# The decay of layer 2 without TensorE: turns by VectorE and memory, a broadcast load, a mask by GpSimd

## The chip, the cores and the metric

The kernel runs on one core of a Trainium2 chip. The metric is the device time of one execution in microseconds (us), taken as the median of several runs. TensorE multiplies matrices into PSUM banks; VectorE, ScalarE and GpSimd work on rows of up to 128 partitions; SyncE (SP) and GpSimd issue loads and stores. In the profile these are PE, DVE, ACT, POOL and SP. Each engine takes its instructions in a fixed order.

## The reference

The reference is a decoder trunk of two layers on 256 tokens of width 1024. Layer 1 is a sparse attention; layer 2, which the change touches, is a chunkwise mLSTM with 8 heads, q and k of 128 and v of 256 per head. What matters here is how its gates weigh the scores:

```python
i_pre = (gi + gate_b[0]).astype(f32).transpose(0, 2, 1)
log_f = jax.nn.log_sigmoid((gf + gate_b[1]).astype(f32)).transpose(0, 2, 1)
b = jnp.cumsum(log_f.reshape(B, H, N, L), axis=-1)
log_d = jnp.where(causal, b[..., :, None] - b[..., None, :] + i_pre[..., None, :], -jnp.inf)
m_j = jnp.maximum(jnp.max(log_d, axis=-1), m_inter)
s = jnp.einsum('bhnjk,bhnsk->bhnjs', q, k) * jnp.exp(log_d - m_j[..., None])
h = num / jnp.maximum(jnp.abs(den), jnp.exp(-m_j))[..., None]
```

The kernel does not chunk: with F the running sum of log_f over all 256 tokens and g = i_pre − F, a key s weighs on a query j by exp(g[s] − M[j]) where M is the running maximum of g (from 0), and by 0 where s is later than j. The floor of the denominator is exp(−(M + F)).

## The kernel before

Tokens lie in two halves of 128. Every weight is loaded by SP's queue into ten buffers (`raw`), split by ScalarE (L164, `wh`, the rounded part) and VectorE (L169, `wl`, the rest), and multiplied by TensorE in three products. `WBUF = 6` pairs of split buffers are kept; a split waits until TensorE has finished with the pair it writes to. The order of each engine's instructions is set at build time by a planner that simulates a timeline and takes what has priority first; `tc.high_priority()` puts its block ahead, `keep_in_program_order` and `issue_after` fix an order.

Between the layers, `turn` (L1092) normalises the tokens and makes the first products of layer 2, among them the 16 gate columns, which VectorE copies to GT (L1240): 128 tokens on the partitions, per half 8 input gates and 8 forget gates. `layer2` (L1282) then does the decay, in rows of 8 partitions (one per head) and 256 tokens, all in one tile `rows` of the tag QK:
- TensorE turns GT into rows (L1332, four transposes); VectorE adds the biases (L1333, L1334).
- log_sigmoid by ScalarE (Abs, Exp, Ln: L1335 to L1338) and VectorE (L1337 to L1343), on 8 x 256.
- VectorE scans F and M and makes −M in two parts in nM (L1344 to L1349).
- TensorE turns g back to columns (L1351), copied to GF (L1352).
- For each head, in bank 2 or 3: TensorE broadcasts the row of −M to 128 partitions with a selecting matrix (L1357), adds the causal mask by two bf16 products with an identity (L1358, L1359); ScalarE writes exp of the sum, with g as its bias, to DT (L1360, L1361).
- M + F, its floor and exp(−(M + F)) (L1363 to L1365), turned to columns by TensorE (L1368).

Around it run the big products: v_unit (values of two heads or one), conv_unit (one convolution over 256 columns of q or k) and later heads. A conv_unit takes a bank from a cycle of six (6, 7, 4, 5, 0, 1), as v_unit does; ScalarE starts `conv` (two buffers, L1380), VectorE adds three shifted terms (L1385) and the end is

```python
            with self.tc.issue_after(last.ins):
                nc.scalar.activation(QK[:, 2 * c : 2 * c + 2], acc, AF.Silu)
```

so a Silu stands behind `last` on ScalarE, and QK, which has the tag of `rows`, is written only when `rows` is free. The order of units is v_unit(2, 2), conv_units 0, 4, 1, 5, v_unit(4, 2), conv_units 2, 6, v_unit(6, 1), conv_units 3, 7; then heads 0 and 1 (`head`, L1389), which read DT at L1395. `factor` (L1414) reads the second half of GF.

Of the kernel before, what the change touches and what calls it, by code (L numbers as in the profile page):

```python
# [7 lines left out]
F32 = mybir.dt.float32  # L8
# [15 lines left out]
class Kernel:  # L24
# [225 lines left out]
    def setup(self):  # L250
# [31 lines left out]
        self.bif = self.T(pc, [8, 2])  # L282
# [17 lines left out]
        self.mask = self.T(pc, [P, P], BF16)  # L300
        self.identb = self.T(pc, [P, P], BF16)
        self.selh = self.T(pc, [P, 8], F32R)
        nc.vector.tensor_copy(self.selh, self.ident[:, 32:40])
        self.identr = self.T(self.p1, [P, P], F32R)
        nc.vector.tensor_copy(self.identr, self.ident)
        nc.vector.tensor_copy(self.selh[0:8], self.ident[0:8, 0:8])

    def late_constants(self):
        g = self.nc.gpsimd
        g.memset(self.int1, 1)  # L310
        g.memset(self.intm, 0x7FFFFFFF)
        m32 = self.T(self.p1, [P, P])
        g.memset(m32, 0.0)
        g.affine_select(m32, m32, pattern=[[1, P]], compare_op=OP.is_ge, fill=-1e30, base=0, channel_multiplier=-1)
        g.tensor_copy(self.mask, m32)
        g.tensor_copy(self.identb, self.ident)
# [775 lines left out]
    def turn(self):  # L1092
# [146 lines left out]
        for a in range(2):  # L1239
            nc.vector.tensor_copy(GT[:, a], bs[a][:, 256:272])  # L1240
# [41 lines left out]
    def layer2(self):  # L1282
# [18 lines left out]
        mask, identb, selh = self.mask, self.identb, self.selh  # L1301
# [19 lines left out]
        rows = self.T(p2, [8, 9, SEQ], tag="QK")  # L1321
        gi, xf, e, u, sp, d, ones, Fc, M = [rows[:, n] for n in range(9)]
        nM = self.T(p2, [P, 384], F32R)
        GF = self.T(p2, [P, 2, 2, 8])
        g.memset(ones, 1.0)
        g.memset(nM.bitcast(F32), 0.0)
        bg, bt = self.bank(2), self.bank(3)
        with self.tc.high_priority():
            for a in range(2):
                for n in range(2):  # L1330
                    c = n * SEQ + a * P
                    nc.tensor.transpose(bg[0:8, c : c + P], GT[:, a, 8 * n : 8 * n + 8], ident)  # L1332
            nc.vector.tensor_scalar(xf, bg[0:8, SEQ:], self.bif[:, 1:2], None, op0=OP.add)  # L1333
            nc.vector.tensor_scalar(gi, bg[0:8, 0:SEQ], self.bif[:, 0:1], None, op0=OP.add)  # L1334
            nc.scalar.activation(e, xf, AF.Abs)  # L1335
            nc.scalar.activation(e, e, AF.Exp, scale=-1.0)
            nc.vector.tensor_scalar(u, e, 1.0, None, op0=OP.add)  # L1337
            nc.scalar.activation(sp, u, AF.Ln)  # L1338
            nc.vector.scalar_tensor_tensor(d, u, -1.0, e, op0=OP.add, op1=OP.subtract)
            nc.vector.reciprocal(u, u)  # L1340
            nc.vector.tensor_tensor(d, d, u, op=OP.mult)
            nc.vector.tensor_sub(sp, sp, d)
            nc.vector.scalar_tensor_tensor(sp, xf, 0.0, sp, op0=OP.min, op1=OP.subtract)  # L1343
            nc.vector.tensor_tensor_scan(Fc, ones, sp, 0.0, OP.mult, OP.add)  # L1344
            nc.vector.tensor_sub(gi, gi, Fc)
            nc.vector.tensor_tensor_scan(M, ones, gi, 0.0, OP.mult, OP.max)
            nc.vector.tensor_scalar(nM[0:8, 0:SEQ], M, -1.0, None, op0=OP.mult)
            nc.vector.scalar_tensor_tensor(nM[32:40, 0:SEQ], M, -1.0, nM[0:8, 0:SEQ].bitcast(F32), op0=OP.mult, op1=OP.subtract)
            nc.vector.tensor_copy(nM[0:40, SEQ:384], nM[0:40, P:SEQ].bitcast(F32))  # L1349
            for a in range(2):  # L1350
                nc.tensor.transpose(bt[:, 8 * a : 8 * a + 8], gi[:, a * P : a * P + P], ident[:8, :8])  # L1351
            nc.vector.tensor_copy(GF[:, 0].rearrange("p a h -> p (a h)"), bt[:, 0:16])  # L1352
        DT = self.T(p2, [P, 8, 384], tag="DT")
        with self.tc.high_priority():
            for h in range(8):
                b = self.bank(2 + h % 2)
                nc.tensor.matmul(b[:, 0:384], selh[:, h : h + 1].to_broadcast([P, P]), nM, start=True, stop=False, skip_group_check=True)  # L1357
                nc.tensor.matmul(b[:, 0:P], identb, mask, start=False, stop=False, skip_group_check=True)  # L1358
                nc.tensor.matmul(b[:, SEQ:384], identb, mask, start=False, stop=True, skip_group_check=True)  # L1359
                nc.scalar.activation(DT[:, h, 0:SEQ], b[:, 0:SEQ], AF.Exp, bias=GF[:, 0, 0, h : h + 1])  # L1360
                last = nc.scalar.activation(DT[:, h, SEQ:384], b[:, SEQ:384], AF.Exp, bias=GF[:, 0, 1, h : h + 1])  # L1361
        v_unit(2, 2)
        nc.vector.tensor_tensor(M, M, Fc, op=OP.add)  # L1363
        nc.vector.tensor_scalar(M, M, -88.0, None, op0=OP.max)
        last = nc.scalar.activation(M, M, AF.Exp, scale=-1.0)  # L1365
        b = self.bank(2)
        for a in range(2):
            nc.tensor.transpose(b[:, 8 * a : 8 * a + 8], M[:, a * P : a * P + P], ident[:8, :8])  # L1368
        nc.vector.tensor_copy(GF[:, 1].rearrange("p a h -> p (a h)"), b[:, 0:16])

# [43 lines left out]
        def factor(b4):  # L1414
            hs = slice(4 * b4, 4 * b4 + 4)
            S = lambda tag: self.T(p2, [P, 2, 4], tag=tag, bufs=2)
            dn, v = S("dn"), S("fv")
            nc.vector.scalar_tensor_tensor(dn, den[:, :, hs], -1.0, den[:, :, hs], op0=OP.mult, op1=OP.max)
            nc.vector.tensor_tensor(dn, dn, GF[:, 1, :, hs], op=OP.max)
            nc.vector.reciprocal(dn, dn)  # L1420
            nc.vector.tensor_tensor(v, ss[:, :, hs], dn, op=OP.mult)
            nc.vector.tensor_tensor(v, v, dn, op=OP.mult)
            nc.vector.tensor_scalar(v, v, 1.0 / 256, 1e-6, op0=OP.mult, op1=OP.add)
            y = self.rsqrt(pc, v.rearrange("p a h -> p (a h)"), 8)
            nc.vector.tensor_tensor(rf[:, :, hs], dn, y.rearrange("p (a h) -> p a h", a=2), op=OP.mult)
# [227 lines left out]
def layout(inputs):  # L1653
# [16 lines left out]
    out["gate_b"] = a["b_gate_b"][0].T  # L1670
# [25 lines left out]
```

## Time and profile before

| what | value |
|---|---|
| median of 3 runs | 427.54 us (427.27 to 427.9) |
| profiled execution, span from first to last instruction | 425.8 us (its only time on the page) |
| TensorE busy | 415.7 us, 98% |
| VectorE busy | 353.7 us, 83% |
| ScalarE busy | 272.0 us, 64% |
| GpSimd busy | 82.1 us, 19% |
| moved by DMA | 94.54 MB, 222 GB/s in the mean |

The span is what the profiler saw; the runs' time also holds what lies around it. Busy time of TensorE is modelled from pipelined matmuls, so that a busy share near 100% says that it was never without work, not that it ran at its peak.

### The profile page before, as it was taken

The numbers are of one execution on the slowest core, as the hardware profiler recorded it, in microseconds if no ns is written. First come the engines' busy times: TensorE is split into PE (matmuls) and PEld (weight loads), VectorE is DVE, ScalarE is ACT, GpSimd is POOL, SyncE is SP. The second block draws the span as 40 slices with busy tenths as digits, with TensorE's granted clock in tenths as the row PEclk, the third lists the DMA queues.
The fourth block names the chain that finished last, engine by engine and source line by source line (L and its number), as shares of the span: only waits on it lengthen the run. The fifth ranks groups of instructions, "written<-read, shape, count | busy, mean of one in ns | idle before, by whom it ended". The sixth has DMA issues, their size and how long they took to land.

```text
span 425.8 us, 7641 instructions
## 1 busy us (share of the span) xinstructions
PE 415.7 (98%) x2701; PEld 359.7 (84%) x2701; DVE 353.7 (83%) x747; ACT 272.0 (64%) x542; POOL 82.1 (19%) x127
## 2 busy tenths in 40 slices
PE   7999999999999999999999999999999999999994
PEld 4899998789778878888998899888888888888884
DVE  6999798999999998979983796889878997458553
ACT  5766693788978964668576865465456454555523
POOL 4000212364586740120000000000000350220000
PEclk9999999999999999999999999999999999999999
DMA  8999986973799678148754366558555687540002
GB/s 313 413 408 407 396 306 192 357 280 107 256 353 391 226 255 307 58 145 295 247 172 168 105 237 190 166 174 264 163 188 197 213 290 229 168 142 0 2 0 99
DMA packets 26886, 94.54 MB, mean 222 GB/s; under 512 B 3072, under 2 KB 3088, under 8 KB 26848
## 3 DMA queue, kind: packets, MB, share of 16 engines
q1 hardware_dynamic: 26208, 92.30, 61.6%
q0 software_dynamic: 352, 0.97, 0.7%
q10 hardware_dynamic: 288, 0.79, 0.5%
q8 instruction: 21, 0.34, 0.3%
q14 instruction: 17, 0.14, 0.1%
HBM read 93.00 MB, written 1.05 MB: 221 GB/s over the span
## 4 chain that ended last, share of the span: by engine, by line
PE 86%; issue 6%; DMA 2%; POOL 2%; DVE 2%; ACT 1%; SPq 1%; DVEq 0%; POOLq 0%; ACTq 0%
PE bank L550 10%; PE bank L548 10%; PE bank L549 10%; PE bank L442 8%; PE bank L1613 6%; PE bank L1611 6%; PE bank L1612 6%; PE bank L1524 5%; PE bank L1045 5%; PE bank L1167 3%; DMA Q<-in_columns 2%; PE bank L808 2%; PE bank L1404 2%; PE bank L825 2%; PE bank L763 2%
## 5 line engine op out<-in xcount | busy, mean ns | idle before, releaser
L169 DVE TENSOR_TENSOR wl<-raw,wh 128x1024 fp32r<-128x1024 f32 (+4 forms) x127 | 139.3, 1112 | 37.3 <-ACT wh L164 36.4
L164 ACT ACTIVATE wh<-raw 128x1024 fp32r<-128x1024 f32 (+4 forms) x127 | 119.4, 957 | 72.9 <-PE bank L550 31.8
L548 PE MATMUL bank<-wh,one 128*128 128x512 f32 (+1 forms) x208 | 76.8, 370 | 0.0
L549 PE MATMUL bank<-wl,one 128*128 128x512 f32 (+1 forms) x208 | 76.3, 367 | 0.0
L550 PE MATMUL bank<-wh,one 128*128 128x512 f32 (+1 forms) x208 | 76.3, 368 | 0.0
L1611 PE MATMUL bank<-one,wh 128*128 128x256 f32 x208 | 59.6, 287 | 0.0
L1613 PE MATMUL bank<-one,wl 128*128 128x256 f32 x208 | 59.2, 285 | 0.1
L1612 PE MATMUL bank<-one,wh 128*128 128x256 f32 x208 | 59.0, 284 | 0.0
L803 POOL TENSOR_SCALAR Pr<-Pr,f 128x128 f32<-128x128 f32 (+1 forms) x42 | 46.7, 1130 | 31.4 <-DVE f L797 25.1
L548 PEld LDWEIGHTS bank<-wh,one 128*128 128x128 f32 x208 | 39.2, 189 | 6.1 <-DVE tz L520 0.2
L550 PEld LDWEIGHTS bank<-wh,one 128*128 128x128 f32 x208 | 39.2, 188 | 6.1
L549 PEld LDWEIGHTS bank<-wl,one 128*128 128x128 f32 x208 | 39.2, 189 | 5.9
L1611 PEld LDWEIGHTS bank<-one,wh 128*128 128x128 f32 x208 | 39.7, 191 | 1.3 <-issue 0.8
L1613 PEld LDWEIGHTS bank<-one,wl 128*128 128x128 f32 x208 | 39.7, 191 | 0.5 <-DVE wl L169 0.3
L1612 PEld LDWEIGHTS bank<-one,wh 128*128 128x128 f32 x208 | 39.7, 191 | 0.1
L789 ACT ACTIVATE Pr<-Pr,mn 128x128 f32<-128x128 f32 (+1 forms) x64 | 28.2, 444 | 4.4 <-DVE mn L782 4.4
L442 PE MATMUL bank<-one,wh 128*128 128x256 f32 x224 | 29.8, 284 | 0.7 <-ACT one L416 0.4
L442 PEld LDWEIGHTS bank<-one,wh 128*128 128x128 f32 x224 | 28.1, 192 | 1.1 <-ACT one L416 0.6
L1487 POOL DMA_DIRECT2D DT<-in_final_g x1 | 0.6, 560 | 131.7 <-DVE pl L1399 131.7
L160 POOL TENSOR_TENSOR raw<-raw,gate 128x256 f32<-128x256 f32 x16 | 15.5, 976 | 47.8 <-DMA raw<-in_out_b 22.5
L1385 DVE SCALAR_TENSOR_TENSOR conv<-bank,one,conv 128x255 f32<-128x255 f32 (+2 forms) x48 | 20.2, 471 | 2.1 <-ACT conv L1380 2.1
L861 DVE CUSTOM_DVE_ANT_0 raw<-raw,one,one 128x1024 f32<-128x1024 f32 x16 | 21.1, 1331 | 0.0
(343 smaller groups left out, 813.6 us busy)
## 6 DMA issues: line engine op xcount, KB each, us to landing
raw<-in_wide SPq DMA_DIRECT2D x44, 512.0 KB, 4.1
raw<-in_units SPq DMA_DIRECT2D x18, 512.0 KB, 3.5
raw<-in_turn SPq DMA_DIRECT2D x16, 512.0 KB, 7.7
raw<-in_gates SPq DMA_DIRECT2D x16, 512.0 KB, 4.7
raw<-in_out_b SPq DMA_DIRECT2D x16, 512.0 KB, 3.8
raw<-in_start SPq DMA_DIRECT2D x8, 512.0 KB, 9.6
Q<-in_columns SPq DMA_DIRECT2D x8, 512.0 KB, 9.6
raw<-in_hidden SPq DMA_DIRECT2D x8, 512.0 KB, 4.2
```

The source lines that it names most:

```text
L164: self.nc.scalar.activation(v(hi), src, AF.Copy)
L169: self.nc.vector.tensor_sub(v(lo), src, v(hi).bitcast(F32))
L442: nc.tensor.matmul(out, w[:, ch * P : ch * P + P], h[:, kk], start=(kk == 0 and m == 0 and ch % 2 == 0), stop=(kk == 7 and m == 2), skip_g ...
L548: nc.tensor.matmul(out, self.hh[:, kk, sl], wh, start=first, stop=False, skip_group_check=True)
L549: nc.tensor.matmul(out, self.hh[:, kk, sl], wl, start=False, stop=False, skip_group_check=True)
L550: nc.tensor.matmul(out, self.hl[:, kk, sl], wh, start=False, stop=last, skip_group_check=True)
L789: nc.scalar.activation(v, v, AF.Exp, bias=mn[:, a, br, j : j + 1], scale=-1.0, accum_out=sm[:, a, br, j : j + 1])
L803: es[br].tensor_scalar(v, v, F[n][:, a, br, j : j + 1], None, op0=OP.mult)
L1045: ins = nc.tensor.matmul(out, l[:, sl], w[:, c0:c1], start=(k == 0 and m == 0), stop=(k == N - 1 and m == 2), skip_group_check=True)
L1611: nc.tensor.matmul(out, wh, self.hh[:, kk], start=first, stop=False, skip_group_check=skip)
L1612: nc.tensor.matmul(out, wh, self.hl[:, kk], start=False, stop=False, skip_group_check=skip)
L1613: nc.tensor.matmul(out, wl, self.hh[:, kk], start=False, stop=last, skip_group_check=skip)
```

## The change

The gates are biased when they leave PSUM (`bif`, the biases, is now loaded to all 128 partitions), and log_sigmoid is made while the tokens are still on the partitions, on 128 x 2 x 8, by GpSimd with Exp and Ln by ScalarE and one reciprocal by VectorE. VectorE's transpose turns blocks of 32 x 32; the blocks go to a scratch tensor in memory (`drawer`) and come back as rows by four loads. The scans stay on VectorE. g goes to memory (`store[0]`) and comes back in blocks for VectorE to turn into GF; −M goes to memory (`shelf`) and is loaded to all 128 partitions of DT. GpSimd writes −1e30 into the masked triangle of two column ranges of DT, and ScalarE takes the exponentials in place. exp(−(M + F)) goes to memory (`store[1]`) and comes back by blocks as g did. `last` is now the last exponential of DT. All new loads and stores are issued by GpSimd. The mask, its bf16 identity and the selecting matrix are no longer made.

```diff
-        self.bif = self.T(pc, [8, 2])
+        self.bif = self.T(pc, [P, 16])
...
-            nc.vector.tensor_copy(GT[:, a], bs[a][:, 256:272])
+            nc.vector.tensor_tensor(GT[:, a], bs[a][:, 256:272], self.bif, op=OP.add)
...
+        rows = self.T(p2, [8, 5, SEQ], tag="QK")
+        gi, xf, ones, Fc, M = [rows[:, n] for n in range(5)]
+        small = self.T(p2, [P, 5, 2, 8])
+        lf, e, u, sp, d = GT[:, :, 8:16], small[:, 0], small[:, 1], small[:, 2], small[:, 3]
+        nM = self.T(p2, [8, 384])
...
+            g.tensor_scalar(d, lf, 0.0, 2.0, op0=OP.min, op1=OP.mult)
+            g.tensor_tensor(d, d, lf, op=OP.subtract)
+            nc.scalar.activation(e, d, AF.Exp)
+            g.tensor_scalar(u, e, 1.0, None, op0=OP.add)
+            nc.scalar.activation(sp, u, AF.Ln)
+            g.tensor_scalar(d, u, -1.0, None, op0=OP.add)
+            g.tensor_tensor(d, d, e, op=OP.subtract)
+            nc.vector.reciprocal(u, u)
+            g.tensor_tensor(d, d, u, op=OP.mult)
+            g.tensor_scalar(lf, lf, 0.0, None, op0=OP.min)
+            g.tensor_tensor(lf, lf, d, op=OP.add)
+            g.tensor_tensor(lf, lf, sp, op=OP.subtract)
+            nc.vector.transpose(turned, GT.rearrange("p a c -> p (a c)"))
+            g.dma_start(drawer, turned)
             for a in range(2):
-                for n in range(2):
-                    c = n * SEQ + a * P
-                    nc.tensor.transpose(bg[0:8, c : c + P], GT[:, a, 8 * n : 8 * n + 8], ident)
...
+                for n, row in enumerate((gi, xf)):
+                    g.dma_start(row[:, a * P : a * P + P].rearrange("h (b k) -> h b k", b=4), drawer.rearrange("(b a n h) k -> a n h b k", b=4, a=2, n=2)[a, n])
+            nc.vector.tensor_tensor_scan(Fc, ones, xf, 0.0, OP.mult, OP.add)
             nc.vector.tensor_sub(gi, gi, Fc)
             nc.vector.tensor_tensor_scan(M, ones, gi, 0.0, OP.mult, OP.max)
...
+            nc.vector.tensor_scalar(nM[:, 0:SEQ], M, -1.0, None, op0=OP.mult)
+            nc.vector.tensor_copy(nM[:, SEQ:384], nM[:, P:SEQ])
+            pin = self.tc.keep_in_program_order
+            pin(g.dma_start(store[0], gi))
+            pin(g.dma_start(shelf, nM))
+            for n in range(4):
+                pin(g.dma_start(blocks[32 * n : 32 * n + 16], store[0].rearrange("h (a k) -> (h a) k", a=2)[:, 32 * n : 32 * n + 32]))
+            pin(g.dma_start(DT.rearrange("p h q -> p (h q)"), shelf.rearrange("h q -> (h q)").unsqueeze(0).partition_broadcast(P)))
+            nc.vector.transpose(GF[:, 0:2].rearrange("p w h a -> p (w h a)"), blocks)
+            for half in (DT[:, :, 0:P], DT[:, :, SEQ:384]):
+                pin(g.affine_select(half, half, pattern=[[0, 8], [1, P]], compare_op=OP.is_ge, fill=-1e30, base=0, channel_multiplier=-1))
+            pin(g.tensor_tensor(M, M, Fc, op=OP.add))
+            g.tensor_scalar(M, M, -88.0, None, op0=OP.max)
+            nc.scalar.activation(M, M, AF.Exp, scale=-1.0)
             for h in range(8):
-                b = self.bank(2 + h % 2)
-                nc.tensor.matmul(b[:, 0:384], selh[:, h : h + 1].to_broadcast([P, P]), nM, start=True, stop=False, skip_group_check=True)
-                nc.tensor.matmul(b[:, 0:P], identb, mask, start=False, stop=False, skip_group_check=True)
-                nc.tensor.matmul(b[:, SEQ:384], identb, mask, start=False, stop=True, skip_group_check=True)
-                nc.scalar.activation(DT[:, h, 0:SEQ], b[:, 0:SEQ], AF.Exp, bias=GF[:, 0, 0, h : h + 1])
-                last = nc.scalar.activation(DT[:, h, SEQ:384], b[:, SEQ:384], AF.Exp, bias=GF[:, 0, 1, h : h + 1])
+                nc.scalar.activation(DT[:, h, 0:SEQ], DT[:, h, 0:SEQ], AF.Exp, bias=GF[:, 0, h, 0:1])
+                last = nc.scalar.activation(DT[:, h, SEQ:384], DT[:, h, SEQ:384], AF.Exp, bias=GF[:, 0, h, 1:2])
+            g.dma_start(store[1], M)
+            for n in range(4):
+                g.dma_start(blocks2[32 * n : 32 * n + 16], store[1].rearrange("h (a k) -> (h a) k", a=2)[:, 32 * n : 32 * n + 32])
+            nc.vector.transpose(GF[:, 2:4].rearrange("p w h a -> p (w h a)"), blocks2)
         v_unit(2, 2)
```

## Rows read from the trace of the kernel before

**Rows 1.** The page: TensorE's and the other engines' busy time, then the granted clock and the moved GB/s in 40 slices of the span.

```profile
PE 415.7 (98%) x2701; PEld 359.7 (84%) x2701; DVE 353.7 (83%) x747; ACT 272.0 (64%) x542; POOL 82.1 (19%) x127
...
PEclk9999999999999999999999999999999999999999
...
GB/s 313 413 408 407 396 306 192 357 280 107 256 353 391 226 255 307 58 145 295 247 172 168 105 237 190 166 174 264 163 188 197 213 290 229 168 142 0 2 0 99
```

**Rows 2.** The view of waits, TensorE alone, over the whole span: who was waited for, us in total, times, longest. The list has eight entries; the first and the latest in time are shown.

```profile
PE bank L248 <- DVE y L263: 1.2, 1, 1.2
...
PE bank L1167 <- DVE one L1154: 0.5, 1, 0.5
```

**Rows 3.** Busy time by stretch: us, then busy us and instructions of PE, PEld, DVE, ACT and POOL, the granted clock, the DMA share, GB/s.

```profile
190.00:210.00 20.00, 20.00 (x115) 17.66 (x115) 18.85 (x28) 14.43 (x18) 0.00 (x0) 1.00 0.81 279
210.00:232.00 22.00, 22.00 (x175) 20.47 (x174) 14.90 (x26) 15.10 (x29) 0.00 (x0) 1.00 0.51 168
232.00:252.00 20.00, 20.00 (x132) 18.15 (x131) 14.74 (x27) 14.57 (x21) 0.00 (x0) 1.00 0.49 154
252.00:270.00 18.00, 18.00 (x152) 18.00 (x151) 14.43 (x23) 9.61 (x14) 0.00 (x0) 1.00 0.64 211
```

**Rows 4.** The timeline of TensorE around the decay's matmuls, in order of time: start us, duration us (of a merged row, from the first start to the last end), instruction, tile, shape, count.

```profile
186.16 0.63 PE L1167 MATMUL bank<-wl,one 128*128 128x512 f32 x2
186.63 0.60 PE L1332 MATMUL bank<-one,one 128*8 128x128 f32 x4
186.98 0.71 PE L1167 MATMUL bank<-wh,one 128*128 128x512 f32 x2
...
212.05 0.28 PE L1611 MATMUL bank<-one,wh 128*128 128x256 f32 x1
...
212.70 0.28 PE L1613 MATMUL bank<-one,wl 128*128 128x256 f32 x1
...
217.97 0.28 PE L1612 MATMUL bank<-one,wh 128*128 128x256 f32 x1
...
218.92 0.28 PE L1611 MATMUL bank<-one,wh 128*128 128x256 f32 x1
...
222.27 0.28 PE L1612 MATMUL bank<-one,wh 128*128 128x256 f32 x1
222.39 0.34 PE L1357 MATMUL bank<-one,one 128*128 128x384 f32 x1
...
222.87 0.28 PE L1611 MATMUL bank<-one,wh 128*128 128x256 f32 x1
...
235.45 0.39 PE L549 MATMUL bank<-wl,one 128*128 128x512 f32 x1
235.77 0.29 PE L1368 MATMUL bank<-one,QK 8*128 8x8 f32 x2
...
236.32 0.40 PE L548 MATMUL bank<-wh,one 128*128 128x512 f32 x1
```

**Rows 5.** The timeline of ScalarE: the logarithm of the gates, the first two heads' exponentials, the table load for the Silu and the first Silus.

```profile
196.09 0.42 ACT L1338 ACTIVATE QK<-QK 8x256 f32<-8x256 f32 x1
...
219.96 0.45 ACT L1360 ACTIVATE DT<-bank,one 128x256 f32<-128x256 f32 x1
...
220.56 0.45 ACT L1360 ACTIVATE DT<-bank,one 128x256 f32<-128x256 f32 x1
...
236.50 1.28 ACT L1387 ACT_TABLE_LOAD   x1
237.79 1.15 ACT L1387 ACTIVATE QK<-conv 128x512 f32<-128x512 f32 x2
...
245.02 0.61 ACT L1387 ACTIVATE QK<-conv 128x512 f32<-128x512 f32 x1
```

**Rows 6.** The timeline of VectorE: the second copy of GT, the first scan and the last copy of −M, and the last term of conv_unit 1.

```profile
186.36 0.17 DVE L1240 COPY one<-bank 128x16 f32<-128x16 f32 x1 [1.26 <-PE bank L1167]
...
208.61 0.67 DVE L1344 TENSOR_TENSOR_SCAN QK<-QK 8x256 f32<-8x256 f32 x1
...
215.03 0.21 DVE L1349 CAST one<-one 40x128 fp32r<-40x128 f32 x1
...
244.14 0.47 DVE L1385 SCALAR_TENSOR_TENSOR conv<-bank,one,conv 128x253 f32<-128x253 f32 x1
```

**Rows 7.** The timeline of TensorE: the first product of v_unit(6, 1).

```profile
252.61 0.28 PE L548 MATMUL bank<-wh,one 128*128 128x256 f32 x1
```

**Rows 8.** The view of DMA issues, three of GpSimd's loads: KB each, median us from issue to landing.

```profile
DT<-in_final_g POOLq DMA_DIRECT2D x1, 512.0 KB, 4.9
...
one<-in_second POOLq DMA_DIRECT2D x1, 28.5 KB, 5.0
...
one<-in_ada_b POOLq DMA_DIRECT2D x1, 4.0 KB, 2.4
```

**Rows 9.** GpSimd's groups of instructions by shape, three of its selects: busy us, mean ns of one, then idle us before. L314 ran at 85 us, L288 and L271 within the first 3 us.

```profile
L314 POOL TENSOR_SCALAR_AFFINE_SELECT one<-one 128x128 f32<-128x128 f32 x1 | 0.8, 772 | 0.1
...
L288 POOL TENSOR_SCALAR_AFFINE_SELECT one<-one 128x256 f32<-128x256 f32 x1 | 0.4, 389 | 0.0
...
L271 POOL TENSOR_SCALAR_AFFINE_SELECT one<-one 128x128 f32<-128x128 f32 x1 | 0.3, 286 | 0.0
```

**Rows 10.** The view of waits, ScalarE alone, from 186 to 270 us: us in total, times, longest.

```profile
ACT wh L164 <- PE bank L1612: 13.5, 10, 2.2
```

More of the change, by code (lines that the diff above doesn't have):

```diff
@@ L235, in build @@
             tc.tile_pool(name="pw", bufs=1) as self.pw,
+            tc.tile_pool(name="pd", bufs=1, space=bass.MemoryType.DRAM) as self.pd,
             tc.tile_pool(name="pp", bufs=1, space=bass.MemoryType.PSUM) as self.pp,
@@ L298, in setup @@
             g.affine_select(self.dc[:, a].rearrange("p i g s -> p (i g) s"), self.dc[:, a].rearrange("p i g s -> p (i g) s"), pattern=[[0, 16], [-16, 16]], compare_op=OP.is_ge, fill=BIG, base=P * a - 31, channel_multiplier=1)
[L300 to L303, printed above, removed]
         self.identr = self.T(self.p1, [P, P], F32R)
         nc.vector.tensor_copy(self.identr, self.ident)
-        nc.vector.tensor_copy(self.selh[0:8], self.ident[0:8, 0:8])
     def late_constants(self):
@@ L311, in late_constants @@
         g.memset(self.intm, 0x7FFFFFFF)
[L312 to L316, printed above, removed]
     def small_loads(self):
@@ L320, in small_loads @@
         self.first_small = [(self.pca[:, 32:89], t["second"])]
-        self.small = [(self.bif, t["gate_b"]), (self.pcb, t["mixer"]), (self.compress, t["compress"])]
+        self.small = [(self.bif, t["gate_b"].partition_broadcast(P)), (self.pcb, t["mixer"]), (self.compress, t["compress"])]
     def layer1(self):
@@ L1299, in values @@
                 nc.vector.tensor_sub(VL[h][:, a, 0:256], s, V[:, a, h, 0:256].bitcast(F32))
-        mask, identb, selh = self.mask, self.identb, self.selh
         def v_unit(h, n):
@@ L1320, in layer2 @@
             values(a, slice(0, 2), vs[a].rearrange("p (h d) -> p h d", h=2))
[L1321 to L1324, printed above, removed]
+        rows = self.T(p2, [8, 5, SEQ], tag="QK")
+        gi, xf, ones, Fc, M = [rows[:, n] for n in range(5)]
+        small = self.T(p2, [P, 5, 2, 8])
+        lf, e, u, sp, d = GT[:, :, 8:16], small[:, 0], small[:, 1], small[:, 2], small[:, 3]
@@ L1325, in layer2 @@
+        nM = self.T(p2, [8, 384])
+        blocks, blocks2 = [self.T(p2, [P, 32]) for _ in range(2)]
+        GF = self.T(p2, [P, 4, 8, 2])
+        DT = self.T(p2, [P, 8, 384], tag="DT")
+        shelf = self.pd.tile([8, 384], F32, name=self.nm("shelf"), tag="shelf")
+        store = self.pd.tile([2, 8, SEQ], F32, name=self.nm("store"), tag="store")
         g.memset(ones, 1.0)
-        g.memset(nM.bitcast(F32), 0.0)
-        bg, bt = self.bank(2), self.bank(3)
+        g.memset(blocks, 0.0)
+        g.memset(blocks2, 0.0)
@@ L1328, in layer2 @@
+        turned = self.T(p2, [P, 32])
+        drawer = self.pd.tile([P, 32], F32, name=self.nm("drawer"), tag="drawer")
         with self.tc.high_priority():
-            for a in range(2):
-                for n in range(2):
-                    c = n * SEQ + a * P
-                    nc.tensor.transpose(bg[0:8, c : c + P], GT[:, a, 8 * n : 8 * n + 8], ident)
-            nc.vector.tensor_scalar(xf, bg[0:8, SEQ:], self.bif[:, 1:2], None, op0=OP.add)
-            nc.vector.tensor_scalar(gi, bg[0:8, 0:SEQ], self.bif[:, 0:1], None, op0=OP.add)
@@ L1335, in layer2 @@
[L1335 to L1343, printed above, removed]
@@ L1344, in layer2 @@
-            nc.vector.tensor_tensor_scan(Fc, ones, sp, 0.0, OP.mult, OP.add)
+            g.tensor_scalar(d, lf, 0.0, 2.0, op0=OP.min, op1=OP.mult)
[6 more added lines that the diff above has]
+            nc.vector.reciprocal(u, u)
@@ L1345, in layer2 @@
+            nc.vector.tensor_tensor_scan(Fc, ones, xf, 0.0, OP.mult, OP.add)
             nc.vector.tensor_sub(gi, gi, Fc)
             nc.vector.tensor_tensor_scan(M, ones, gi, 0.0, OP.mult, OP.max)
[L1347 to L1351, printed above, removed]
@@ L1352, in layer2 @@
-            nc.vector.tensor_copy(GF[:, 0].rearrange("p a h -> p (a h)"), bt[:, 0:16])
-        DT = self.T(p2, [P, 8, 384], tag="DT")
-        with self.tc.high_priority():
-            for h in range(8):
-                b = self.bank(2 + h % 2)
-                nc.tensor.matmul(b[:, 0:384], selh[:, h : h + 1].to_broadcast([P, P]), nM, start=True, stop=False, skip_group_check=True)
-                nc.tensor.matmul(b[:, 0:P], identb, mask, start=False, stop=False, skip_group_check=True)
-                nc.tensor.matmul(b[:, SEQ:384], identb, mask, start=False, stop=True, skip_group_check=True)
-                nc.scalar.activation(DT[:, h, 0:SEQ], b[:, 0:SEQ], AF.Exp, bias=GF[:, 0, 0, h : h + 1])
-                last = nc.scalar.activation(DT[:, h, SEQ:384], b[:, SEQ:384], AF.Exp, bias=GF[:, 0, 1, h : h + 1])
@@ L1362, in layer2 @@
-        v_unit(2, 2)
[L1363 to L1369, printed above, removed]
+            nc.vector.tensor_scalar(nM[:, 0:SEQ], M, -1.0, None, op0=OP.mult)
@@ L1418, in factor @@
             nc.vector.scalar_tensor_tensor(dn, den[:, :, hs], -1.0, den[:, :, hs], op0=OP.mult, op1=OP.max)
-            nc.vector.tensor_tensor(dn, dn, GF[:, 1, :, hs], op=OP.max)
+            nc.vector.tensor_tensor(dn, dn, GF[:, 2, hs].rearrange("p h a -> p a h"), op=OP.max)
             nc.vector.reciprocal(dn, dn)
@@ L1669, in layout @@
         np.stack([w2[0], w2[0]], axis=2).reshape(P, 256), w2[1].reshape(P, 128)], axis=1)
-    out["gate_b"] = a["b_gate_b"][0].T
+    out["gate_b"] = a["b_gate_b"][0].reshape(1, 16)
     columns = a["ada_w"][0][:, : 2 * D].reshape(D, 2, KC, P).transpose(2, 1, 3, 0)
```

## Prediction

> **What bounds the kernel now.** I read the page's engine shares first. TensorE is busy for 98% of the span, the next engine for 83%, and the granted clock is at its top in every slice, the 2.4 GHz level [rows 1]. Busy need not mean bound, so I went to TensorE's waits: all of them together are under 5 us, and the last one is at L1167, the product in front of layer 2 [rows 2]. Then the stretches of layer 2 that hold the decay and what follows it: TensorE is busy for the whole of each, 22.00 of 22.00 us and so on, while VectorE, ScalarE and the DMA all have room and GpSimd does nothing at all [rows 3]. So between 190 and 270 us the time is the sum of TensorE's slots. A slot taken out there is worth its full length, provided nothing new makes TensorE wait.
>
> **What goes from TensorE.** A matmul's own duration overlaps its neighbours, so I price each removed group by start times: from the matmul before it to a matmul behind it, less the steps that these take without it (0.12 us for 256 columns, 0.23 us for 512) [rows 4].
> - The four turns of the gates, L1332: 186.16 to 186.98 is 0.82, less two steps of 0.23: 0.36.
> - The two turns of L1351: 212.05 to 212.70 is 0.65, less 0.24: 0.41.
> - Heads 0 and 1 (L1357 to L1359, six matmuls): 217.97 to 218.92 is 0.95, less 0.24: 0.71.
> - Each later head: 222.27 to 222.87 is 0.60, less 0.24: 0.36; six of them, 2.16.
> - The two turns of L1368: 235.45 to 236.32 is 0.87, less 0.46: 0.41.
> Sum: 0.36 + 0.41 + 0.71 + 2.16 + 0.41 = 4.05 us.
>
> **What comes in its place, and by when it must be done.** None of the new work is on TensorE; it can cost only by being late. The first user of the decay is head 0's product near 270 us, too far off to matter. The near user is hidden in an ordering: conv_unit's Silu is issued after `last`, and writes the tile with the tag QK, whose earlier tenant is `rows`. Before, `last` is the exponential of M; after, it is the last of the sixteen exponentials of DT, and `rows` is free only once the store of M has landed. Behind the Silu stand the two `conv` buffers, behind these the banks of the convolutions. Now the Silu's table load starts at 236.50, the first two Silus at 237.79, the third, which closes conv_unit 1, at 245.02 [rows 5], just after its last VectorE term (244.14 + 0.47) [rows 6]. From Silu to free bank is 244.6 − 237.8 = 6.8 us. That bank, bank 0, is taken next by v_unit(6, 1), whose first product starts at 252.61 [rows 7]. With 4.05 us gone ahead of it the need comes at 248.6. So the first Silu must start by 248.6 − 6.8 = 241.8 us; each us later is a us that TensorE stands still.
>
> The chain to that point, each step with its bounds:
> - GT is complete at 186.36 + 0.17 = 186.5 [rows 6]. Ten tiny GpSimd operations, Exp and Ln with a table load each, and VectorE's reciprocal follow. Ln ended at 196.09 + 0.42 = 196.5 before, between the same weight splits [rows 5]; I keep that. Floor: 186.5 + 2 x (1.28 + 0.42) + 0.5 = 190.4; ceiling 198.5, two more splits ahead of it. The turn by VectorE, not seen in the trace, is one small instruction behind at most one split of 1.2 us: done at 198 (191 to 200).
> - First trip through memory (`drawer`): GpSimd's loads land 2.4 us after issue (4 KB) to 5.0 us [rows 8]. The DMA share in this stretch is 0.81 [rows 3], so I take 4.0: 202.
> - Second trip: four loads, each issue takes GpSimd 0.57, so the last leaves 1.7 later: 202 + 1.7 + 4.0 = 207.7. Before, the first scan ran at 208.61, so the rows reach the scan no later than they did: fewer steps stood in VectorE's queue.
> - Scans to the last copy took 215.03 + 0.21 − 208.61 = 6.6 us with splits in between [rows 6]; the five instructions alone are 2.3. I take 4.0: 211.7.
> - Third trip (`shelf`), 4.0: 215.7. The small loads into `blocks` issue inside it.
> - The load of DT: 128 x 8 x 384 x 4 bytes are 1.57 MB. No row shows such a load on this queue. Nearest is final_g, 0.52 MB in 4.9 us [rows 8]. Low end: 1.57 MB at 413 GB/s, the best slice of the span [rows 1], and 2.4: 6.2. High end: three times 4.9: 14.7. I take 2.4 + 3 x (4.9 − 2.4) = 9.9, nearest to the one broadcast row: 226.
> - Two selects by GpSimd of 128 x 1024 each. Rows show only 128 x 128: 0.286 at the start, 0.772 at 85 us [rows 9]. Low end 1.0 (a slope of 0.8 ns an element from the 256-wide one, 0.389, also there), high end 2.7 times that; I take 1.5 each: 229.
> - Exponentials: 0.60 from one head's start to the next (219.96 to 220.56) [rows 5], so 4.8 for eight, and 2.6 for the splits and M between: 236.5. Table for Silu, 1.3: 237.8.
> So the Silu comes out where it is now, 4.0 us ahead of the need. M's own branch (sum, exponential, store) leaves GpSimd behind the selects and, with 1.5 us to the store and 4.0 for it, frees `rows` at 234.5, inside the exponentials. All low ends give 217, all high ends 252.
>
> The rule that speaks against this: the Trainium skill, GPSIMD Engine Reference, Key points, says that GpSimd shares its SBUF interfaces with VectorE and contends with VectorE's two-input instructions. The trace agrees, 0.772 against 0.286 us for the same select. By the rule both selects take their high end, the Silu starts at 240.2, and the sum stays as it is.
>
> **Added waits in front of others.** VectorE stands at the scan until the rows land, ScalarE at the first exponential until the selects are done, and the weight splits queue behind both, which TensorE needs. Cover: six buffer pairs are kept. ScalarE's splits wait 13.5 us in all for TensorE to free one [rows 10], so the pairs are full, some five parts ahead; a part of 24 steps of 0.12 lasts 2.9 us. That is 14 us, less about 3 for the split itself: 11 us of blocking cost nothing, all beyond costs in full. GpSimd holds nothing that others wait for here. The raw loads on SP's queue lose some 4 to 5 us of DMA time to the 1.57 MB, in a stretch where the share is 0.51 [rows 3].
>
> **Costed at nothing:** the constants that go (mask, its bf16 identity, selh) and the wider load of the gate biases, which lie in layer 1 off TensorE; the add in place of the copy of GT; the many small VectorE instructions that go, as VectorE isn't the bound. If the cover of GpSimd's idleness were gone, these are tenths of a us each.
>
> **Sum.** 425.8 − 4.05 = 421.75 for the span. The page gives no other time for this execution; the median of the runs, 427.54, lies 1.74 above the span. Forecast: 423.5 us.
>
> **Rivals.**
> - *Late Silu.* The four trips, the broadcast and the selects run towards their high ends, and TensorE stands at bank 0. For it: five of the steps have no equal in the trace and lie in one line. Against: the estimate has 4.0 us to spare. A Silu at 244 gives 425.7; at 245.8 everything is given back, 427.5, and from there it is slower: at 249, 430.7, at the high end 433.7.
> - *Blocked splits.* ScalarE stands at the first exponential for longer than its 11 us, since its order was fixed for earlier data. 5 us beyond the cover: 428.5. Against: loads of this size land within 10 us.
> - *Nothing gained.* TensorE's slots go, but it is paced by the splits or the loads and idles as much: 427.5. Against: no wait of TensorE after L1167, and full buffers.
>
> **Chances.** Saving kept to within 0.7 us: 0.56. Late Silu that eats part of it, still over 0.86 us (0.2%, about what a measurement of this kernel can tell from no change) faster: 0.14; that eats about all: 0.08; that makes it slower: 0.13. Nothing gained: 0.04. Blocked splits: 0.05. Faster 0.70, same 0.12, slower 0.18. The likeliest case has 422.7 to 424.2 for itself; the range runs from 422.4 to 428.5, which leaves out the worse half of the late cases.
>
> **What would show it.** No L1332, L1351, L1357 to L1359 or L1368 kind on TensorE, and 4 us earlier starts from 240 us on. Right: no idle time of TensorE before v_unit(6, 1), the first Silu before 242. Wrong: TensorE waiting there for VectorE's convolution, or for a split behind an exponential; DT landing after 231.

## The result, and the profile after

The changed kernel takes 423.74 us in the median of 4 runs (423.27 to 424.21) against 427.43 for the kernel before in the same session: a ratio of 0.9911, 95% interval 0.9898 to 0.9924, so 3.2 to 4.4 us faster. The span fell from 425.8 to 421.5.

The page after: engine shares, then the granted clock in 40 slices.

```profile
PE 412.3 (98%) x2669; PEld 357.2 (85%) x2669; DVE 348.6 (83%) x736; ACT 270.8 (64%) x541; POOL 96.6 (23%) x154
...
PEclk9999999999999999999999999999999999999998
```

TensorE lost 32 matmuls and 3.4 us of busy time and kept its 98% and its clock [rows 1]; GpSimd gained 14.5 us. The waits of TensorE, whole span; the list again has eight entries, here the first and the latest in time:

```profile
PE bank L249 <- DVE y L264: 1.2, 1, 1.2
PE bank L1158 <- DVE one L1145: 0.5, 1, 0.5
```

No new wait in layer 2: as in [rows 2], the latest stands in front of it, and from 186 us on the view lists none. The stretches of [rows 3], in the changed kernel:

```profile
190.00:210.00 20.00, 20.00 (x118) 17.78 (x117) 13.94 (x22) 13.93 (x18) 5.24 (x11) 1.00 0.84 276
210.00:232.00 22.00, 22.00 (x162) 20.96 (x161) 13.90 (x24) 13.75 (x26) 7.77 (x11) 1.00 0.63 241
232.00:252.00 20.00, 20.00 (x150) 19.14 (x149) 16.75 (x29) 17.19 (x26) 2.55 (x5) 1.00 0.53 173
252.00:270.00 18.00, 18.00 (x138) 17.34 (x137) 16.63 (x29) 11.01 (x17) 0.00 (x0) 1.00 0.69 224
```

TensorE is still busy for the whole of each. GpSimd's column, empty before in all four, is filled in three of them; the DMA share rose (0.51 to 0.63 in the second stretch, where DT is loaded), and VectorE's busy time fell in the first, from 18.85 to 13.94 us. Where the time went is read from three marks on TensorE: the first product of the last gate unit, the first of v_unit(2, 2), the first of v_unit(6, 1). Before, the third is [rows 7]; the first two are:

```profile
181.67 2.17 PE L1167 MATMUL bank<-wh,one 128*128 128x272 f32 x12 [0.51 <-DVE one L1154]
...
191.63 0.39 PE L548 MATMUL bank<-wh,one 128*128 128x512 f32 x1
```

and after:

```profile
181.29 2.17 PE L1158 MATMUL bank<-wh,one 128*128 128x272 f32 x12 [0.49 <-DVE one L1145]
...
191.13 0.39 PE L539 MATMUL bank<-wh,one 128*128 128x512 f32 x1
...
248.37 0.28 PE L539 MATMUL bank<-wh,one 128*128 128x256 f32 x1
```

From the first mark to the second, 191.63 − 181.67 = 9.96 us became 191.13 − 181.29 = 9.84: the gates' turns gave 0.12. From the second to the third, 252.61 − 191.63 = 60.98 became 248.37 − 191.13 = 57.24: 3.74. The other 0.38 of the span's 4.3 lies before the first mark, in layer 1, and changes from profile to profile: its last product group (L1158) begins at 172.5 here, at 173.2 and 173.4 in two kernels below that differ from this one only in layer 2.

The chain that stands in TensorE's place, on GpSimd and, for the turn, VectorE (in order of time):

```profile
186.62 1.12 POOL L1328 TENSOR_TENSOR one<-one,one 128x16 f32<-128x16 f32 x1
...
194.31 0.22 POOL L1337 TENSOR_TENSOR one<-one,one 128x16 f32<-128x16 f32 x1
194.61 1.20 POOL L1338 TENSOR_TENSOR one<-one,one 128x16 f32<-128x16 f32 x1
197.81 0.20 DVE L1339 STREAM_TRANSPOSE one<-one 128x32 f32<-128x32 f32 x1
198.30 0.66 POOL L1340 DMA_DIRECT2D drawer<-one  x1 [2.49 <-DVE num L1290]
202.16 2.21 POOL L1343 DMA_DIRECT2D QK<-drawer  x4 [3.20 <-DMA drawer<-one]
...
215.06 0.55 POOL L1354 DMA_DIRECT2D DT<-shelf  x1
224.82 2.65 POOL L1357 TENSOR_SCALAR_AFFINE_SELECT DT<-DT 128x1024 f32<-128x1024 f32 x2 [9.21 <-DMA DT<-shelf]
...
233.66 0.60 POOL L1364 DMA_DIRECT2D store<-QK  x1 [4.53 <-ACT QK L1360]
235.68 1.95 POOL L1366 DMA_DIRECT2D one<-store  x4 [1.42 <-DMA store<-QK]
```

on ScalarE:

```profile
226.46 3.31 ACT L1362 ACTIVATE DT<-DT,one 128x256 f32<-128x256 f32 x8 [0.33 <-POOL DT L1357]
229.68 2.44 ACT L1363 ACTIVATE DT<-DT,one 128x128 f32<-128x128 f32 x8
...
232.97 0.40 ACT L1360 ACTIVATE QK<-QK 8x256 f32<-8x256 f32 x1
...
235.45 1.28 ACT L1386 ACT_TABLE_LOAD   x1 [0.17 <-issue]
236.74 1.15 ACT L1386 ACTIVATE QK<-conv 128x512 f32<-128x512 f32 x2
...
244.69 0.63 ACT L1386 ACTIVATE QK<-conv 128x512 f32<-128x512 f32 x1 [1.17 <-DVE conv L1384]
```

and its trips through memory (KB each, median us from issue to landing):

```profile
DT<-shelf POOLq DMA_DIRECT2D x1, 1536.0 KB, 9.7
...
QK<-drawer POOLq DMA_DIRECT2D x4, 4.0 KB, 4.9
...
drawer<-one POOLq DMA_DIRECT2D x1, 16.0 KB, 3.6
shelf<-one POOLq DMA_DIRECT2D x1, 12.0 KB, 2.1
```

These rows are one line of waits: where a row has a bracket, it says how long the engine stood idle before it and what ended that, mostly the step before it or that step's DMA (at 198.30 it names a subtraction of VectorE beside the turn, which ended at 198.0). It ends with Silus at 236.74. The third, at 244.69, starts when VectorE's last term of conv_unit 1 is done; that term, which ended at 244.6, also frees bank 0, 3.8 us before v_unit(6, 1) takes it.

### The profile page after: what moved, and what is told of

Read it like the earlier page. It is cut to its first block, busy times and chain, and to the rows that moved or that the text cites. A ratio compares the mean times of both kernels' runs of the same rounds, so it can differ in the third digit from the quotient of the medians.

```text
span 421.5 us, 7600 instructions
## 1 busy us (share of the span) xinstructions
PE 412.3 (98%) x2669; PEld 357.2 (85%) x2669; DVE 348.6 (83%) x736; ACT 270.8 (64%) x541; POOL 96.6 (23%) x154
## 4 chain that ended last, share of the span: by engine, by line
PE 84%; issue 5%; DMA 4%; POOL 2%; DVE 2%; ACT 1%; SPq 0%; DVEq 0%; POOLq 0%
PE bank L539 10%; PE bank L541 10%; PE bank L540 10%; PE bank L433 7%; PE bank L1612 6%; PE bank L1610 6%; PE bank L1611 6%; PE bank L1523 5%; PE bank L1036 5%; PE bank L1158 3%; DMA Q<-in_columns 3%; PE bank L799 2%; PE bank L1403 2%; PE bank L816 2%; PE bank L754 2%
## 5 line engine op out<-in xcount | busy, mean ns | idle before, releaser
L160 POOL TENSOR_TENSOR raw<-raw,gate 128x256 f32<-128x256 f32 x16 | 13.6, 858 | 49.7 <-DMA raw<-in_out_b 24.9
L773 DVE CUSTOM_DVE_ANT_0 Pr<-bank,one 128x128 f32<-128x128 f32 (+1 forms) x64 | 18.7, 348 | 0.0
```

## The experiments

The theory: TensorE's slots are the currency and the new chain is free as long as it ends before bank 0 is wanted. The rivals: the gain comes from elsewhere (VectorE's shorter list, layer 1); the chain already costs; its first user is head 0, so that it has 20 us to spare; or the splits queued behind the exponentials hurt first.

**The slots put back as idle work.** Eight products in front of each of four conv_units:

```diff
+            if c in (0, 4, 1, 5):
+                spare = self.bank(2 + c % 2)
+                for _ in range(8):
+                    nc.tensor.matmul(spare[:, 0:SEQ], self.hh[:, 0, 0:P], self.hh[:, 1], start=True, stop=True)
```

> The changed kernel with 32 products of 256 columns (0.12 us each by their steps) put back on TensorE, eight in front of each of conv_units 0, 4, 1 and 5, into banks 2 and 3, read by nobody. If the gain is TensorE's removed slots and nothing else: 32 x 0.12 = 3.84 us are given back, 423.7 + 3.8 = 427.5, no change against before. If it came from VectorE's shorter list or from layer 1, and TensorE has room: it stays at 423.7, 0.991 of before.

427.06 us (ratio 0.9985, 0.9975 to 0.9994): 3.3 of the 3.84 came back. Nearly all the gain is slots; for VectorE's list, still as short as in the changed kernel, at most the 0.6 us are left by which this kernel beats the one before in the same session (427.70). Part of the missing half us has a place. The planner put 24 of the 32 products before 190 us, and there TensorE has a hole in the changed kernel: two steps of 0.23 us take 0.69 instead of 0.46, and the weight loads show what they wait for (timeline, then the view of waits, weight loads alone, 186 to 420 us):

```profile
185.76 0.62 PE L1158 MATMUL bank<-wl,one 128*128 128x512 f32 x2
186.45 3.48 PE L1158 MATMUL bank<-wh,one 128*128 128x512 f32 x14
...
PEld bank L1158 <- ACT wh L164: 0.5, 1, 0.5
```

By the starts the hole is 0.23 us. With the idle products the wait is not listed: they fill it, as the gates' turns did before the change. The rest of the half us has no place.

**DT by TensorE again, the rest as changed.** The 24 matmuls of the heads return; load and selects go.

```diff
-            pin(g.dma_start(shelf, nM))
-            pin(g.dma_start(DT.rearrange("p h q -> p (h q)"), shelf.rearrange("h q -> (h q)").unsqueeze(0).partition_broadcast(P)))
-            for half in (DT[:, :, 0:P], DT[:, :, SEQ:384]):
-                pin(g.affine_select(half, half, pattern=[[0, 8], [1, P]], compare_op=OP.is_ge, fill=-1e30, base=0, channel_multiplier=-1))
+                b = self.bank(2 + h % 2)
+                nc.tensor.matmul(b[:, 0:384], selh[:, h : h + 1].to_broadcast([P, P]), nM, start=True, stop=False, skip_group_check=True)
+                nc.tensor.matmul(b[:, 0:P], identb, mask, start=False, stop=False, skip_group_check=True)
+                nc.tensor.matmul(b[:, SEQ:384], identb, mask, start=False, stop=True, skip_group_check=True)
```

> The changed kernel, but DT made by TensorE as before (per head one product that broadcasts the row of maxima and two for the mask; no broadcast load, no selects); gates, scans, turns of g and M stay as changed, the constants are back. If slots are the currency: 24 matmuls by their steps, 0.71 + 2.16 = 2.87 us come back, 426.6. If the broadcast by a load costs something of its own through contention or waits, less than 2.87 comes back. If the gain is elsewhere: 423.7.

428.22 us (1.0012), 4.5 above the changed kernel, not 2.9. The trace gave 0.4 to a wait of the first of these matmuls for the row of maxima, and the rest to something unforeseen: products that the edit doesn't touch had become slower. The returning constants had moved the split buffers by 544 bytes, from address 82048 in a partition to 82592. So I moved addresses alone. Unused bytes were put behind `bif`, in the changed kernel and in this one; they move the split buffers and every other buffer behind them, while the tokens, the other operand of these products, stay at one address in all the kernels:

```diff
         self.bif = self.T(pc, [P, 16])
+        self.T(pc, [P, 8])
```

(8 for 32 bytes; 16, 24, 48 and 56 words in the others.)

> The changed kernel with one unused tile of 32 bytes per partition put behind bif, so that every buffer after it lies 32 bytes on; no instruction differs. In the run with the broadcast on TensorE the buffers lay at addresses of 32 modulo 64 and the step from one 512-column product to the next was 0.233 us, against 0.227 in the changed kernel, where they lie at 0 modulo 64. If the address is the cause: the step becomes 0.233, some 480 steps of that kind in layer 2 cost 6 ns each, 2 to 3 us in all, 426. If it was the edit itself: 423.7, step 0.227.

425.09 us (0.9939, 0.9923 to 0.9956), 1.35 slower with no instruction changed; the interval just meets that of the changed kernel, so the steps are the better sign. TensorE's timeline in v_unit(2, 2), changed kernel, eleven starts:

```profile
192.72 0.39 PE L539 MATMUL bank<-wh,one 128*128 128x512 f32 x1
...
194.99 0.39 PE L540 MATMUL bank<-wl,one 128*128 128x512 f32 x1
```

and with 32 bytes, ten starts:

```profile
192.73 0.40 PE L541 MATMUL bank<-wl,one 128*128 128x512 f32 x1
...
194.83 0.39 PE L541 MATMUL bank<-wl,one 128*128 128x512 f32 x1
```

2.27 in 10 steps is 0.227; 2.10 in 9 steps is 0.233. The direction was right, the price expected, 2 to 3 us, too high: the 256-column products, which it left out, became faster, 0.118 instead of 0.120.

> The broadcast on TensorE again, with the same 32 bytes put in, so that the buffers lie at 0 modulo 64. If the address cost it the excess: step 0.227 and 423.7 + 2.87 for the 24 matmuls + 0.4 for the wait that the trace showed at their first = 427.0. If 24 matmuls and their waits cost more than their steps: it stays at 428.2.

424.82 us (0.9933): a miss, 2.2 below what was expected. The step was 0.229, not 0.227, so 0 modulo 64 is not the rule. And the 256-column products ran faster than in any other kernel here, at 0.113 instead of 0.120, up to 254 us; from there, with the granted clock at 1.00 on both sides, at 0.118. Each pair of rows spans 24 steps:

```profile
251.84 0.28 PE L550 MATMUL bank<-wh,one 128*128 128x256 f32 x1
...
254.56 0.28 PE L1623 MATMUL bank<-one,wh 128*128 128x256 f32 x1
...
257.38 0.28 PE L1623 MATMUL bank<-one,wh 128*128 128x256 f32 x1
...
260.21 0.28 PE L1623 MATMUL bank<-one,wh 128*128 128x256 f32 x1
```

2.72 in 24 steps is 0.113, 2.83 is 0.118. Some 320 steps at 0.113 are worth about 1.5 us against 0.118 (an estimate from these steps).

> The broadcast on TensorE again with 96 bytes put in, so that the split buffers lie at 0 modulo 128 like those of the changed kernel: the clean price of the 24 matmuls. By their steps 2.87, and 0.4 of wait at the first: 423.7 + 3.3 = 427.0, step of 512 columns 0.227. If the broadcast load and the selects gain less than the slots (contention elsewhere): under 426.

428.01 us (1.0003), step 0.232: 0 modulo 128 isn't the rule either.

> The broadcast on TensorE once more, with 224 unused bytes, so that the split buffers lie at 128 modulo 256, as in the kernel before and in the changed one. So far two kernels with the same address modulo 256 had the same step (128: 0.227 us for 512 columns; 160: 0.233; 192: 0.229), and the one at 0 modulo 256 had 0.232 though it is at 0 modulo 128. If that is the rule: step 0.227, and 423.7 + 2.87 + up to 0.4 of wait = 426.6 to 427.0. If the slots cost more than their steps: 428.

426.70 us (0.9977, 0.9966 to 0.9987), step 0.227: 2.96 above the changed kernel, where 2.87 had been read from the steps. At this address the broadcast and the mask on TensorE cost their slots and no more: from v_unit(2, 2) to v_unit(6, 1) the profile has 251.47 − 191.42 = 60.05 us against 57.24, 2.81 more, and TensorE does not wait after layer 1. Two other pairs with equal address are on record. At 160 modulo 256 it is 428.22 against 425.09, 3.13 with the wait of 0.4. At 192 it is 424.82 against 423.08 (the last kernel of this group), only 1.74; there the kernel with the broadcast had the 0.113 steps, and their estimated 1.5 us are about what is missing.

> The changed kernel with 192 unused bytes, split buffers at 64 modulo 256, the one multiple of 64 not yet seen. If the step goes with the address modulo 256 it takes a value of its own, somewhere in 0.227 to 0.233, and the time lies between 422 and 426; if 64 and 192 are alike (64 modulo 128), step 0.229 and 423.1, as with 64 bytes.

424.90 us (0.9937), step 0.233, and 0.118 for 256 columns: not a value of its own but that of 160, and 64 and 192 are not alike. All kernels together, by the address of the split buffers modulo 256 (mean steps in v_unit(2, 2), and in the 256-column products from the convolutions to v_unit(6, 1) and conv_units 3 and 7, from the timelines):

| address modulo 256 | kernels | 512 columns | 256 columns |
|---|---|---|---|
| 128 | before, changed, idle products, selects thrice, 224 bytes | 0.227 | 0.120 |
| 192 | changed + 64 bytes | 0.229 | 0.118 |
| 192 | broadcast + 32 bytes | 0.229 | 0.113 up to 254 us, then 0.118 |
| 64 | changed + 192 bytes | 0.233 | 0.118 |
| 0 | broadcast + 96 bytes | 0.232 | 0.119 |
| 160 | broadcast, changed + 32 bytes | 0.233 | 0.118 |

Before and changed kernel share the first row, so their comparison is not touched by this.

> The changed kernel with 64 unused bytes per partition behind bif, so that the split buffers lie at 64 modulo 128 (before and changed kernel: 0 modulo 128); no instruction differs. The run with the broadcast on TensorE at that address had layer 1 over at 171.4 instead of 172.5, a step of 0.113 us for 256-column products early in the convolutions (0.120 before) and of 0.229 for 512 columns (0.227). If these go with the address: 1.1 us in layer 1 and some 2 us in the convolutions gained, 1 us lost in the wide products, 421.5 to 422, faster than both kernels. If they go with the edit: 423.7.

423.08 us (0.9884, 0.9868 to 0.9901): the best median here. The interval meets that of the changed kernel (0.9898 to 0.9924), and the profiled span, 421.9, is not below its 421.5, so that this version beats the kernel before, by 4.2 to 5.7 us, and whether it beats the changed one stays open. Layer 1 began its last group at 172.9 and the 256-column step was 0.118 throughout: neither the early 171.4 nor the 0.113 went with the address, and neither shows itself in another run, so what made them stays open.

**The chain made later.** The selects are repeated; a second pass writes what is there.

```diff
-            for half in (DT[:, :, 0:P], DT[:, :, SEQ:384]):
+            for half in 3 * (DT[:, :, 0:P], DT[:, :, SEQ:384]):
```

> The changed kernel with the two selects done three times over (the result is the same): the exponentials of DT and the Silus behind them move by 2 x 2.65 = 5.3 us. If bank 0 for v_unit(6, 1) is the first thing that needs the decay: it came free at 244.6 and was wanted at 248.4, 3.8 us of slack, so about 1.5 us are lost, 425.2, and TensorE waits for a VectorE term of a convolution near 248 us. If head 0 at 265 us is the first user: no cost, 423.7. If the weight splits behind the exponentials are what hurts first: TensorE waits for a split, for 2 us or more, before 248 us.

426.26 us (0.9979, 0.9956 to 1.0002). TensorE's timeline has one wait in layer 2:

```profile
252.19 0.39 PE L539 MATMUL bank<-wh,one 128*128 128x256 f32 x1 [1.43 <-DVE conv L1384]
```

It is the product and the cause that were foretold: v_unit(6, 1), VectorE's convolution. That the length, 1.4 us, comes near the 1.5 expected is in part luck: v_unit(6, 1) starts 3.1 us late by the marks (22.42 us behind the first product of v_unit(4, 2) in the changed kernel, 252.19 − 226.63 = 25.56 here), and the planner, which saw the later chain, had filled the rest with the score products of heads 0 and 1 and two products of the next unit. The median rose by 2.5; 0.7 more of the profiled span lies in front of layer 2. The ten runs spread from 425.2 to 429.2: the four above 427 have a mean granted clock of 0.993 or 0.994, the six others 0.997 or more, and only one of the six was profiled, so the price beyond the wait is not settled. Twice over (`2 *`):

> The selects done twice, 2.65 us later. If the slack in front of bank 0 is 3.8 us: no cost, 423.7, and no wait of TensorE after layer 1. If any delay of the decay costs (the change's chain already sets the time): 426.4.

424.48 us (0.9925, 0.991 to 0.9941), 0.7 more, though within the intervals. But the wait is there:

```profile
249.29 0.59 PE L1391 MATMUL bank<-QK 128*128 128x256 f32 x2
249.72 0.38 PE L1392 MATMUL bank<-QK 128*128 128x128 f32 x2
250.75 0.35 PE L539 MATMUL bank<-wh,one 128*128 128x256 f32 x1 [0.64 <-DVE conv L1384]
```

Here too the planner put head 0's score products (L1391, L1392) ahead of v_unit(6, 1), which without them would have started at 249.29; bank 0 came free at 250.6, so it was 1.3 late. The 3.8 us of slack are used up, by a delay of which only 2.65 were put in. ScalarE's rows say why:

```profile
239.92 1.28 ACT L1386 ACT_TABLE_LOAD   x1
241.21 1.15 ACT L1386 ACTIVATE QK<-conv 128x512 f32<-128x512 f32 x2
...
250.69 0.63 ACT L1386 ACTIVATE QK<-conv 128x512 f32<-128x512 f32 x1 [2.23 <-DVE conv L1384]
```

The first Silu moved by 4.5 us where 2.65 were put in: the load of DT was issued 0.4 later and took 10.9 us instead of 9.7. From the Silu to the free bank it takes 9.4 us instead of 7.9: the splits and values that were held back stand in VectorE's and ScalarE's queues ahead of the convolutions. The bank came 6.0 us later in all; TensorE itself was 0.9 later out of layer 1, and 6.0 − 0.9 − 3.8 are the 1.3. Five times over (`5 *`):

> The same with the selects five times over, 10.6 us later. Bank 0: 10.6 - 3.8 = 6.8 us lost, 430.5, slower than before, TensorE waiting for a VectorE term of a convolution near 248 us. Head 0 as first user: 423.7. Splits: ScalarE's gap between two splits was 223.2 to 232.0, 8.9 us, and becomes 19.5; the buffers hold some 14 us, less 3 for a split, so 8 us lost, 432, TensorE waiting for splits.

431.24 us (1.0082, 1.0055 to 1.0109), slower than the kernel before. TensorE's waits in layer 2:

```profile
PE bank L1610 <- ACT wh L164: 2.1, 1, 2.1
PE bank L1612 <- DVE wl L169: 1.9, 1, 1.9
PE bank L1391 <- ACT QK L1386: 1.4, 1, 1.4
```

Now the splits starve it as well, 4.0 of 5.4 us; the planner had again put head 0 ahead of v_unit(6, 1), so that it is head 0 that waits for a Silu. And a second price, in the stretches (us, busy us of PE, PEld, DVE, ACT, POOL, clock, DMA):

```profile
252.00:256.00 4.00, 0.50 (x2) 0.30 (x2) 4.00 (x9) 2.89 (x5) 0.00 (x0) 0.95 0.57 204
256.00:260.00 4.00, 3.65 (x17) 3.65 (x18) 4.00 (x10) 2.10 (x4) 0.00 (x0) 0.50 0.43 131
260.00:264.00 4.00, 4.00 (x26) 4.00 (x26) 3.33 (x8) 2.73 (x5) 0.00 (x0) 0.70 0.45 131
```

After 4 us in which TensorE worked for 0.5, the granted clock is 0.50, the 1.2 GHz level, and comes back within the third row: 2.0 + 1.2 = 3.2 us at full speed are gone. (The profiled run is the slowest of the four, 432.55.)

**The Silus taken off the chain's end.** With the selects three times over, M's sum, exponential and store go in front of the selects, and `last` is M's exponential again:

```diff
+            pin(g.tensor_tensor(M, M, Fc, op=OP.add))
+            g.tensor_scalar(M, M, -88.0, None, op0=OP.max)
+            last = nc.scalar.activation(M, M, AF.Exp, scale=-1.0)
+            pin(g.dma_start(store[1], M))
...
-                last = nc.scalar.activation(DT[:, h, SEQ:384], DT[:, h, SEQ:384], AF.Exp, bias=GF[:, 0, h, 1:2])
+                nc.scalar.activation(DT[:, h, SEQ:384], DT[:, h, SEQ:384], AF.Exp, bias=GF[:, 0, h, 1:2])
```

> The selects three times over (5.3 us late, 426.3 when tried), but with M's sum, exponential and store put in front of the selects and the Silus ordered behind M's exponential, as before the change, instead of behind the last exponential of DT. If the Silu's order is the link: TensorE's 1.4 us wait for the convolution at v_unit(6, 1) goes, 424 to 424.7 (one more table load on ScalarE). If it is the splits queued behind the exponentials: still 426.

424.39 us (0.9921, 0.9906 to 0.9936), and TensorE has no wait after layer 1. DT itself comes much later than in the changed kernel, and no product waits for it:

```profile
238.00 3.31 ACT L1365 ACTIVATE DT<-DT,one 128x256 f32<-128x256 f32 x8
```

These exponentials began at 226.46 in the changed kernel. The same 5.3 us in the selects cost 2.5 with the Silus behind the exponentials and 0.7, within the intervals, without: what hangs on the chain's end is the Silu, not head 0. Three things are not separated here. The edit takes away both of the Silu's ties, the order behind `last` and the tile that M's store frees (in the changed kernel the last exponential of DT ended at 232.1 and the store had landed by 235.7). And with the Silus done meanwhile ScalarE no longer stands idle in front of the exponentials, so the splits are not held back either. That they are not what TensorE waited for at this delay is read from the wait in the run with three selects alone, which names a convolution and no split.

## Why the prediction was right

- *What bounds the kernel.* Right: slots given back as idle work returned 3.3 us, and at the changed kernel's address modulo 256 the 24 matmuls of the heads returned 2.96.
- *What goes from TensorE.* The sum of 4.05 measured 3.86 between the marks. L1351, the heads and L1368 were put at 3.69 and gave 3.74. The four turns of the gates were put at 0.36 and gave 0.12: this term was mis-sized, since I read it between two neighbours as if TensorE had work waiting; without the turns it waits there for ScalarE's split, 0.23 us. That the span fell by 4.3 owes 0.38 to layer 1.
- *The chain.* The turn was put at 198 and ended at 198.0; DT's load was put at 9.9 us and took 9.7; the selects at 3.0 and took 2.65; the first Silu at 237.8 and came at 236.74. That the end comes so near is in part luck, for single steps were off in both directions: Ln ended at 193.5, not 196.5, the loads of rows took 4.9, not 4.0, and the store into `shelf` 2.1, not 4.0. The exponentials took 5.6 us in one piece and ended at 232.1, where I had spread them over 7.5 and ended them at 236.5; but then ScalarE did three splits and M's exponential before the table load, 3.4 us, where I had counted 2.6 among the exponentials. M's store, which was to free `rows` at 234.5 inside the exponentials, was issued behind them and had landed by 235.7.
- *By when it must be done.* The place was right (`last`, Silu, bank 0, v_unit(6, 1)), shown by the wait at that product with a later chain and by its absence with the Silus freed. The spare time, put at 4.0 us, was 3.8, but out of two misses that cancel: 6.8 us from Silu to bank were read from a kernel without held-back splits, and it took 7.9; the Silu came 1.1 earlier than put. Nor is "each us later is a us that TensorE stands still" the price: with the chain later, this stretch grew to 9.4, and 2.65 us in the selects were enough to use the spare time up.
- *Added waits.* No split came late in the changed kernel; at 10.6 us of delay they did, so the cover is finite, as put, but the 11 us were not measured by themselves.
- *The rule against it.* GpSimd beside VectorE: a 128 x 16 two-input operation took 0.22 us at 194.31 (L1337, an add), while VectorE stood still, and another 1.20 us at 194.61 (L1338, a subtract), after VectorE had begun a split's subtraction, which reads two inputs:

```profile
194.50 2.39 DVE L169 TENSOR_TENSOR wl<-raw,wh 128x1024 fp32r<-128x1024 f32 x2 [0.63 <-ACT wh L164]
```

  The Trainium skill, GPSIMD Engine Reference, Key points, says that GpSimd shares its SBUF interfaces with VectorE and contends with VectorE's instructions that have two SBUF inputs; these rows agree. The selects, which would have cost most, took 1.3 each: VectorE had one subtraction beside them, until 225.48, and then stood idle, its splits held back behind ScalarE's exponentials. That was not foreseen, so that the low price of the selects is luck.
- *Rivals.* Late Silu is real: 2.65 us more in the selects are enough for a wait, and 10.6 make the kernel slower, as its far end said. Blocked splits come later than it. Nothing gained: refuted.

## What to carry to other kernels

On a kernel whose TensorE never waits, price a removed matmul by the starts of its neighbours, but look whether the engine would have had work at that moment: a small matmul in front of a late operand costs less than its slot, 0.12 instead of 0.36 us here. Work moved off TensorE is free only up to its first user, and that can be an instruction that is merely ordered behind it; look for such orders, for shared buffers, and for the queue that builds up while it is awaited: 2.65 us put in arrived as 6.0 at the bank here. When an edit changes the size of any tile, compare the steps of untouched matmuls, narrow and wide ones, before explaining its time.

## What was not expected of the hardware

The step from one of the big products to the next goes with where in a partition the buffers behind `bif`, the split buffers among them, lie: 0.227 to 0.233 us for 512 columns, the clock at full, and the kernels with equal address modulo 256 agree in it, whatever else was edited (eight of them at 128, two each at 160 and 192; 0 and 64 were seen once). With no instruction changed the medians run from 423.08 to 425.09. The tokens lie at one address in all of them, so it is not their place that differs; whether it is the read of the split weights or other buffers that were moved with them was not tried. For 256 columns the step is 0.118 to 0.120, and the address does not settle it: the broadcast with 32 bytes had 0.113 up to 254 us and 0.118 from there, where another kernel with the same address modulo 256 has 0.118 throughout. What sets that one stays open.
